# Low parts of the linear-attention input weights: from a VectorE subtract to a negated copy with an adding transfer

## The chip, the cores and the metric

The kernel runs on one core of a Trainium2 chip. The metric is device time in microseconds (us) of one execution; the median of the runs is compared. TensorE (PE) multiplies matrices and PEld is its loading of weights; VectorE (DVE), ScalarE (ACT) and GpSimd (POOL) work elementwise; SyncE (SP) issues most transfers (DMA), ScalarE a few, and GpSimd those that add to what lies at their destination.

## The reference

One inference step of a two-layer decoder with D = 1024, for 512 prompt tokens and 8 decode rows, everything in f32. Layer 0 mixes tokens by windowed attention, layer 1 by gated linear attention (GLA); each is followed by a ConvFFN with 2816 channels and by layer norms. The part that matters here is layer 1's mixer with 4 heads:

```python
def gla_mix(x, s0, w_in, w_a1, w_a2, b_a, norm_g, w_o):
    proj = x @ w_in            # q, k: 128 columns per head; v, g: 256 per head
    ...
    log_a = jax.nn.log_sigmoid(((x @ w_a1) @ w_a2 + b_a).astype(jnp.float32)) / GLA_TAU
    ...
    o, s_new = gla_recurrence(q, k, v, log_a, s0, min(GLA_CHUNK, T))
    o = o * lax.rsqrt(jnp.mean(jnp.square(o), -1, keepdims=True) + NORM_EPS) * norm_g
    o = (o * jax.nn.silu(g)).reshape(B, T, GLA_DV)
    return o @ w_o, s_new
```

## The kernel before

**Products.** Every f32 weight block is split into a high part `wh` (the f32r copy of it) and a low part `wl` (the rest), and so are the activations; a product is high x high, high x low and low x high, three matmuls for each of 8 pieces of the contraction, 24 in all (`product`: lines 231, 233 and 235; line 238 where all low parts stand behind the high parts). The tokens go in two groups, a (256 columns) and b (256 + 8 decode rows).

**Units.** The work is a list of units, each with one weight block of 128 x 1024 values (512 KB). Units 0 to 9 are attention's q, k, v, 10 to 17 its output, 18 to 65 the first ConvFFN (8 single units of gate and value, 18 paired ones, each of which makes one low by transfer in the helper `upper`, and the down-projections), 66 the low-rank decay, **67 to 90 the input weights of the linear attention**, 91 to 98 its output, and from 99 the second ConvFFN. A head of the linear attention has six units: q, k, v0, v1, g0, g1 (67 to 72 are head 0, 73 to 78 head 1, and so on).

**Order.** `order` lets group b follow group a by 4 or 5 units. When b has finished unit u, its slot (6 slots of `wh` and `wl`) is released and `load_next` emits the load of a later unit, `load_unit` (line 175): SP loads the block into one of two raw buffers (184), ScalarE makes the high part (189), and then comes the low part: a VectorE subtract (195), or, for three kinds of units, `low_by_dma` (200, 201), which lets ScalarE write the negated high part and GpSimd issue a transfer that reads the block from DRAM again and adds it. The instructions are not run in the order in which they are emitted: a planner at build time simulates them with its own costs and fixes an order for each engine, so that matmuls of several products can be interleaved. On the chip each engine takes its own list strictly in order.

**Late units.** The first units after a layer norm (here 67 to 71) are marked late; they go through `parts` (line 203), which already uses `low_by_dma` while a norm in certain places is under way (line 211 to 214).

**Around it.** `gla_g` makes the gate: an exponential on ScalarE (1173), plus 1 on GpSimd (`de`, 1174), a reciprocal (1175) and `sg` (1177) on VectorE, which frees the PSUM buffer of the product; later `sg` is scaled by the transposed attention output (1185). `gla_decay` makes the decay (996 to 1014). `gla_sample` advances the states of the decode rows: SP loads values broadcast over the partitions (`vb`, 1155), ScalarE scales the state (1159), VectorE adds the outer product (`sgla`, 1160), SP stores it (1161) and loads the next head's (1019).

Of the kernel before, what the change touches and what calls it, by code (L numbers as in the profile page):

```python
# [99 lines left out]
class Net:  # L100
# [74 lines left out]
    def load_unit(self, u, pieces=1, late=False):  # L175
        src, nt = self.units[u][0], self.units[u][1]
        nc = self.nc
        if nt == 0:
            return self.load_rank(u)
        r = self.raw.tile([P, KD * P], F32, name="raw")  # L180
        h, l = ((self.wx if u == self.extra else self.wts).tile([P, KD * P], F32R, name=name) for name in ("wh", "wl"))
        n = nt * P // pieces
        for c in (slice(i * n, (i + 1) * n) for i in range(pieces)):
            nc.sync.dma_start(out=r[:, c], in_=src[:, c])
            if late:
                self.spawn(self.parts(u, h[:, c], l[:, c], r[:, c], src[:, c]), 1)
                continue
            if u >= HIACT:
                nc.scalar.activation(h[:, c], r[:, c], AF.Copy)  # L189
            else:  # L190
                nc.gpsimd.tensor_scalar(h[:, c], r[:, c], 1.0, 0.0, op0=ALU.mult, op1=ALU.add)
            if self.units[u][2] in (self.ffn_down2, self.ffn_gate, self.ffn_value):
                self.low_by_dma(l[:, c], h[:, c], src[:, c])
            else:
                nc.vector.tensor_tensor(l[:, c], r[:, c], h[:, c].bitcast(F32), op=ALU.subtract)  # L195
        self.w[u] = (h, l)
# [1269 lines left out]
```

## Time and profile before

| | |
|---|---|
| median of 3 runs | 1103.12 us (1101.35 to 1103.88) |
| profiled execution: time / span | 1103.29 us / 1101.5 us |
| mean granted TensorE clock | 0.993 |
| HBM read / written | 153.24 MB / 8.47 MB |

The profile is one execution. The span goes from its first instruction to its last. In rows of instruction groups stand the line, engine, operation, output<-input, shape and count, then busy time and mean (ns), then the idle time of the engine before them and what ended it. In rows of waits: engine, line, what it waited for, us in total, times, longest. In rows of the timeline: start, duration (both us), engine, line, operation, and in brackets the idle time before with its releaser. In rows of windows: the stretch, its length, busy time and instructions of PE, PEld, DVE, ACT and POOL, the granted clock, the share of time in which the 16 transfer engines are busy, and GB/s. Busy time of a matmul is its own duration; matmuls overlap.

### The profile page before, as it was taken

What the parts mean: (1) busy time and instruction counts of PE and PEld (TensorE: products, weight loads), DVE (VectorE), ACT (ScalarE), POOL (GpSimd) and SP (SyncE); (2) the same over time, 40 slices, a digit from 0 to 9 for tenths busy, and PEclk for the clock granted to TensorE, in tenths of its full rate; (3) what the DMA queues carried; (4) which work ended last, traced back from release to release, by engine and by line L of the source; (5) the groups of instructions that cost most, each with busy time, mean ns of one, the idle gap of its engine ahead of it and who ended that gap; (6) DMA issues with size and microseconds to landing.
All of it is one profiled execution on the core that took longest, in us unless ns stands there. A gap on an engine that the chain in (4) does not pass through costs nothing.

```text
span 1101.5 us, 23798 instructions
## 1 busy us (share of the span) xinstructions
PE 1058.3 (96%) x9174; PEld 1030.9 (94%) x9174; DVE 881.2 (80%) x1797; ACT 663.1 (60%) x1308; POOL 308.2 (28%) x512
## 2 busy tenths in 40 slices
PE   8999999899999999999899999999999999999996
PEld 7998899899999999999899899899899999999995
DVE  7897668987778888978667777778987788788975
ACT  5677667866665565647445556467866555655643
POOL 4576562311111110274111100363311111110163
PEclk9999999999999999999999999999999999999998
DMA  7454047687777775438125354558687777774412
GB/s 228 150 171 126 21 135 198 169 193 183 177 181 173 178 166 119 148 106 206 58 74 150 124 177 134 158 172 210 156 192 178 183 174 175 172 190 115 131 50 78
DMA packets 65472, 167.44 MB, mean 152 GB/s; under 512 B 8104, under 2 KB 28624, under 8 KB 65360
## 3 DMA queue, kind: packets, MB, share of 16 engines
q1 hardware_dynamic: 50960, 119.47, 33.7%
q0 software_dynamic: 12240, 44.57, 23.1%
q10 hardware_dynamic: 2160, 1.89, 0.6%
q8 instruction: 72, 1.18, 0.4%
q14 instruction: 40, 0.33, 0.1%
HBM read 153.24 MB, written 8.47 MB: 147 GB/s over the span
## 4 chain that ended last, share of the span: by engine, by line
PE 65%; DVE 13%; DMA 11%; ACT 5%; issue 4%; POOL 1%; SPq 0%; DVEq 0%; ACTq 0%; POOLq 0%
PE widep L303 7%; PE widep L304 7%; PE widep L305 7%; PE accp L231 6%; PE accp L233 6%; PE accp L235 5%; PE widep L898 5%; PE widep L899 5%; PE widep L900 5%; DMA vb<-dv 3%; DMA wl<-in_w_up 3%; DMA raw<-in_w_up 2%; PE accp L917 2%; PE accp L238 1%; PE onep L304 1%
## 5 line engine op out<-in xcount | busy, mean ns | idle before, releaser
L308 ACT ACTIVATE wh<-raw 128x1024 fp32r<-128x1024 f32 x72 | 76.3, 1060 | 103.6 <-PE widep L899 65.8
L189 ACT ACTIVATE wh<-raw 128x1024 fp32r<-128x1024 f32 (+1 forms) x92 | 96.0, 1047 | 59.9 <-PE accp L233 25.9
L303 PE MATMUL widep<-th,wh 128*128 128x264 f32 (+1 forms) x432 | 119.1, 276 | 0.0
L304 PE MATMUL widep<-tl,wh 128*128 128x264 f32 (+1 forms) x432 | 119.1, 276 | 0.0
L305 PE MATMUL widep<-th,wl 128*128 128x264 f32 (+1 forms) x432 | 119.1, 276 | 0.0
L231 PE MATMUL accp<-xh_b,wh 128*128 128x264 f32 x400 | 113.0, 283 | 5.2 <-DVE hprod L801 3.4
L231 PE MATMUL accp<-xs_a,wh 128*128 128x256 f32 x400 | 106.2, 285 | 5.9 <-DVE sg L1177 2.5
L235 PE MATMUL accp<-xh_b,wl 128*128 128x264 f32 x400 | 111.5, 279 | 0.0
L233 PE MATMUL accp<-xl_b,wh 128*128 128x264 f32 x384 | 107.4, 280 | 0.0
L201 POOL DMA_DIRECT2D wl<-in_w_down x28 | 24.3, 868 | 288.3 <-ACT wl L200 276.1
L233 PE MATMUL accp<-xs_a,wh 128*128 128x256 f32 x384 | 103.0, 284 | 0.3
L309 DVE TENSOR_TENSOR wl<-raw,wh 128x1024 fp32r<-128x1024 f32 x72 | 88.2, 1225 | 9.4 <-ACT wh L308 9.3
L195 DVE TENSOR_TENSOR wl<-raw,wh 128x1024 fp32r<-128x1024 f32 (+2 forms) x64 | 79.3, 1247 | 13.4 <-ACT wh L189 12.5
L200 ACT ACTIVATE wl<-wh 128x1024 fp32r<-128x1024 f32 x85 | 89.0, 1050 | 0.9
L827 DVE TENSOR_TENSOR merged<-widep,conv 128x528 f32<-128x528 f32 x72 | 37.4, 562 | 58.3 <-PE widep L305 58.3
L231 PEld LDWEIGHTS accp<-xs_a,wh 128*128 128x128 f32 x400 | 76.7, 195 | 7.7 <-ACT wh L189 3.0
L303 PEld LDWEIGHTS widep<-th,wh 128*128 128x128 f32 x432 | 82.1, 190 | 0.1
L304 PEld LDWEIGHTS widep<-tl,wh 128*128 128x128 f32 x432 | 82.1, 190 | 0.0
L305 PEld LDWEIGHTS widep<-th,wl 128*128 128x128 f32 x432 | 82.1, 190 | 0.0
L231 PEld LDWEIGHTS accp<-xh_b,wh 128*128 128x128 f32 x400 | 75.7, 189 | 6.7 <-DVE hprod L801 4.0
L303 PE MATMUL widep<-xh_b,wh 128*128 128x264 f32 x288 | 79.6, 276 | 0.0
L304 PE MATMUL widep<-xl_b,wh 128*128 128x264 f32 x288 | 79.5, 276 | 0.0
(419 smaller groups left out, 4165.8 us busy)
## 6 DMA issues: line engine op xcount, KB each, us to landing
raw<-in_w_up SPq DMA_DIRECT2D x88, 512.0 KB, 3.9
wl<-in_w_up POOLq DMA_DIRECT2D x52, 512.0 KB, 6.6
raw<-in_w_down SPq DMA_DIRECT2D x44, 512.0 KB, 3.7
wl<-in_w_down POOLq DMA_DIRECT2D x28, 512.0 KB, 6.4
raw<-in_w_gla SPq DMA_DIRECT2D x24, 512.0 KB, 3.5
raw<-in_w_mix_o SPq DMA_DIRECT2D x16, 512.0 KB, 3.9
qs<-hl SPq DMA_DIRECT2D x64, 64.0 KB, 2.1
sgla<-in_state_gla SPq DMA_DIRECT2D x16, 256.0 KB, 3.0
```

Of the source, the lines that this page charges most:

```text
L189: nc.scalar.activation(h[:, c], r[:, c], AF.Copy)
L195: nc.vector.tensor_tensor(l[:, c], r[:, c], h[:, c].bitcast(F32), op=ALU.subtract)
L200: self.nc.scalar.activation(l, h.bitcast(F32), AF.Copy, scale=-1.0)
L231: nc.tensor.matmul(o, h[:, ks], xh, start=k == 0, stop=False)
L233: nc.tensor.matmul(o, h[:, ks], xl, start=False, stop=False)
L235: nc.tensor.matmul(o, l[:, ks], xh, start=False, stop=not tail and k == nt - 1)
L303: self.nc.tensor.matmul(o, h[:, ks], rh, start=k == 0, stop=False)
L304: self.nc.tensor.matmul(o, h[:, ks], rl, start=False, stop=False)
L305: self.final = self.nc.tensor.matmul(o, l[:, ks], rh, start=False, stop=k == KD // 2 - 1).ins
L308: self.nc.scalar.activation(hi, src, AF.Copy)
L309: self.nc.vector.tensor_tensor(lo, src, hi.bitcast(F32), op=ALU.subtract)
L898: nc.tensor.matmul(o, h[:, ks], rh, start=k == 0, stop=False)
```

## The change

The condition on line 192 names the kinds of units whose low part is made by `low_by_dma`. Four kinds are added: the query, key, value and gate units of the linear attention.

```diff
-            if self.units[u][2] in (self.ffn_down2, self.ffn_gate, self.ffn_value):
+            if self.units[u][2] in (self.ffn_down2, self.ffn_gate, self.ffn_value, self.gla_q, self.gla_k, self.gla_v, self.gla_g):
                 self.low_by_dma(l[:, c], h[:, c], src[:, c])
             else:
                 nc.vector.tensor_tensor(l[:, c], r[:, c], h[:, c].bitcast(F32), op=ALU.subtract)
```

The helper that it calls is as before:

```python
def low_by_dma(self, l, h, src):
    self.nc.scalar.activation(l, h.bitcast(F32), AF.Copy, scale=-1.0)
    self.nc.gpsimd.dma_start(out=l, in_=src, accum_op=ALU.add)
```

Units 67 to 71 do not pass line 192. For the others the low part is now made from the high part and DRAM, and the raw buffer is read by the high part's copy alone.

## The prediction

> **What bounds the kernel now.** I read the page's busy shares, then the windows of the stage that the change touches, then what TensorE waits for there.
>
> ```profile
> PE 1058.3 (96%) x9174; PEld 1030.9 (94%) x9174; DVE 881.2 (80%) x1797; ACT 663.1 (60%) x1308; POOL 308.2 (28%) x512
> ```
> ```profile
> core 0: us, PE busy (x) PEld busy (x) DVE busy (x) ACT busy (x) POOL busy (x), PEclk, DMA share, GB/s
> 530.00:690.00 160.00, 154.52 (x1282) 147.40 (x1281) 114.61 (x281) 82.83 (x214) 18.52 (x30) 0.99 0.41 127
> 540.00:550.00 10.00, 7.46 (x44) 6.90 (x43) 7.64 (x17) 5.12 (x15) 4.12 (x9) 0.83 0.24 89
> 586.00:598.00 12.00, 12.00 (x106) 11.90 (x105) 11.32 (x32) 7.93 (x22) 0.87 (x2) 1.00 0.57 173
> 598.00:610.00 12.00, 10.18 (x89) 9.90 (x87) 5.51 (x12) 3.88 (x9) 0.00 (x0) 1.00 0.75 210
> 640.00:650.00 10.00, 8.87 (x79) 8.68 (x79) 5.71 (x16) 4.33 (x10) 0.00 (x0) 1.00 0.73 215
> ```
>
> TensorE (PE) is busy for 96% of the span. In the linear attention (here 530 to 690 us) it is idle for 160 - 154.5 = 5.5 us. Between 540 and 550 us the granted clock is 0.83, worth 10 x 0.17 = 1.7 us. A change to that stage's weights can therefore win about 7 us at most; it can lose more. VectorE (DVE) is at 114.6 of 160 us (72%), ScalarE (ACT) at 52%, and the transfers have 0.41 of their engines. The waits of TensorE between 500 and 690 us, in us, times and longest, are all of these:
>
> ```profile
> PE accp L231 <- DVE sg L1177: 2.5, 1, 2.5
> PE accp L238 <- DMA wl<-in_w_gla: 1.9, 1, 1.9
> PE tp L1065 <- DVE sg L1185: 1.8, 1, 1.8
> PE accp L231 <- ACT wh L189: 1.4, 1, 1.4
> PE tp L1181 <- ACT on L1105: 1.1, 1, 1.1
> ```
>
> Two of the five are for VectorE, and one is already for a low part made by transfer.
>
> **What the change moves.** Each of the 24 units (67 to 90) has one 512 KB weight block. The rows of its low parts and high parts, with count, busy time and mean, and of the transfers that exist already:
>
> ```profile
> L195 DVE TENSOR_TENSOR wl<-raw,wh 128x1024 fp32r<-128x1024 f32 x19 | 23.4, 1229 | 7.2 <-ACT wh L189 6.8 <-PE accp L235 0.3
> ```
> ```profile
> L200 ACT ACTIVATE wl<-wh 128x1024 fp32r<-128x1024 f32 x85 | 89.0, 1050 | 0.9
> ```
> ```profile
> L201 POOL DMA_DIRECT2D wl<-in_w_up x52: 856/865/1028, 154.1 to 1025.4; - x52
> L201 POOL DMA_DIRECT2D wl<-in_w_gla x5: 865/880/881, 501.7 to 515.4; - x5
> ...
> DMA to landing us min/median/max: 5.2/6.6/10.5
> ```
>
> Units 67 to 71 go through another branch, and their five lows are transfers already (x5). The change acts on the other 19. It takes 19 x 1.229 = 23.4 us from VectorE, adds 19 x 1.050 = 20.0 us to ScalarE and 19 x 0.865 = 16.4 us of issuing to GpSimd (POOL), and reads each block a second time. On the transfer engines:
>
> ```profile
> q1 hardware_dynamic: 50960, 119.47, 33.7%
> q0 software_dynamic: 12240, 44.57, 23.1%
> ```
>
> q0 carries the 85 lows: 0.231 x 1101.5 / 85 = 3.0 us of all 16 engines each, so 19 cost 57 us of them. ScalarE rises from 82.8 to about 103 of 160 us, which does not bound it.
>
> *Term 1, VectorE's relief.* The longest wait, 2.5 us before 544.24, ends on a gate (sg) that stands right behind a subtract:
>
> ```profile
> 542.64 1.21 DVE L195 TENSOR_TENSOR wl<-raw,wh 128x1024 fp32r<-128x1024 f32 x1
> 543.77 0.41 DVE L1177 TENSOR_TENSOR sg<-accp,de 128x256 f32<-128x256 f32 x1
> ```
> ```profile
> 544.24 0.53 PE L231 MATMUL accp<-xs_a,wh 128*128 128x256 f32 x1 [2.54 <-DVE sg L1177]
> ```
>
> Without it sg can start 1.2 us earlier. I take 1.2 of the 2.5 us (bounds 0, if the extra ScalarE copy delays the gate's exponential by as much, and 2.5). The clock drop right after this wait, 1.7 us, I take as gone with a wait half as long: -2.9 us in all. The Trainium skill's page "TensorE: Matmul & The Clock Gate", section "HAM oscillation — how this bites in real kernels", says that idle gaps over about 3.4 us bring the slow clock. The trace disagrees: its gap was 2.5 us, and the slow clock followed. By the page's rule the drop would not hang on this gap, the term would be -1.2, and the sum 1.7 us higher.
>
> *Term 2, lows that come late.* A weight slot is freed when group b has done with it; six slots turn round, so unit u waits for b's product of unit u-6, and a's product of u follows soon. For unit 75: the last low matmul of unit 69, the high part, and a's first use of the new low:
>
> ```profile
> 551.46 0.28 PE L235 MATMUL accp<-xh_b,wl 128*128 128x264 f32 x1
> 557.84 0.28 PE L235 MATMUL accp<-xs_a,wl 128*128 128x256 f32 x1
> ```
> ```profile
> 552.06 1.04 ACT L189 ACTIVATE wh<-raw 128x1024 fp32r<-128x1024 f32 x1
> ```
>
> From the slot's release (551.74) to that use is 6.1 us, the shortest of 18 such spans (units 73 to 90; mean 8.3, longest 11.8). The first and the last:
>
> ```profile
> 536.13 0.28 PE L235 MATMUL accp<-xh_b,wl 128*128 128x264 f32 x1
> 544.77 0.42 PE L235 MATMUL accp<-xs_a,wl 128*128 128x256 f32 x1
> ...
> 664.56 0.38 PE L235 MATMUL accp<-xh_b,wl 128*128 128x264 f32 x1
> 672.33 0.28 PE L235 MATMUL accp<-xs_a,wl 128*128 128x256 f32 x1
> ```
>
> The old path needs 0.3 + 1.04 + 1.2 = 2.6 us. The new one needs 0.3 + 1.04 + 1.05 + 0.1 + 6.6 (median landing) = 9.1 us, more than 13 of the 18 spans. In the old order of matmuls TensorE would stand still. But the planner that fixes the order at build time knows that transfers take time, and can run b's product while a's low is missing. It has done so in the first ConvFFN, where b's product (xh_b) runs ahead of a's last low:
>
> ```profile
> 184.34 0.28 PE L235 MATMUL accp<-xh_b,wl 128*128 128x264 f32 x1
> ...
> 188.04 0.38 PE L238 MATMUL accp<-xs_a,wl 128*128 128x256 f32 x2
> ```
>
> What was lost there nevertheless, in the whole run, is the 1.9 us above and
>
> ```profile
> PE accp L238 <- DMA wl<-in_w_up: 2.5, 3, 1.2
> PE accp L235 <- DMA wl<-in_w_up: 0.6, 2, 0.4
> ```
>
> That is 5.0 us over 21 single units whose low is a transfer (52 - 36 of paired units, and 5): 0.24 us each. These are the nearest rows, and 19 x 0.24 = 4.5 us. Bounds: 0 if the planner moves b far enough ahead; if it moves nothing, each stall lengthens the next unit's span by its own length, so about every second unit stalls: 0.4 + 3.0 + 2.1 + 2.9 + 0.1 + 2.1 + 2.4 + 0.2 + 1.6 = 14.8 us. The Trainium skill's page "DMA: Bandwidth & Descriptors", section "Anatomy of one DMA — SWDGE (gpsimd) path", gives 2.0 us plus bytes over 436,000, an estimated 3.2 us for a block; by it the path would be 5.7 us, under every span, and this term 0. The trace disagrees: no landing is under 5.2 us.
>
> *Term 3, the transfers of the decode rows.* VectorE's state updates wait for the broadcast values (vb), and the subtract is not what holds them:
>
> ```profile
> 601.67 0.88 DVE L1160 SCALAR_TENSOR_TENSOR sgla<-vb,kraw,sgla 128x256 f32<-128x256 f32 x2 [3.19 <-DMA vb<-dv]
> 602.47 0.48 DVE L1185 SCALAR_TENSOR_TENSOR sg<-tp,par,sg 128x256 f32<-128x256 f32 x1
> 602.86 1.22 DVE L195 TENSOR_TENSOR wl<-raw,wh 128x1024 fp32r<-128x1024 f32 x1
> ...
> 607.58 0.88 DVE L1160 SCALAR_TENSOR_TENSOR sgla<-vb,kraw,sgla 128x256 f32<-128x256 f32 x2 [3.17 <-DMA vb<-dv]
> 608.38 0.48 DVE L1185 SCALAR_TENSOR_TENSOR sg<-tp,par,sg 128x256 f32<-128x256 f32 x1
> ```
>
> Behind the second wait stands the sg that TensorE waited 1.8 us for. In these 24 us (586 to 610) the transfers are busy for 0.57 x 12 + 0.75 x 12 = 15.8 us; three of the 19 lows fall in them (of units 80 to 82; the last one's subtract is in the fence) and make 15.8 + 9.0 = 24.8 of 24. So vb lands later by part of a low. The same stage of the next head is the 640 to 650 window (0.73), whose 1.1 us wait stands there. The last two heads' stages come when the weights are loaded, or nearly. I take 2.0 us for each of two heads, 4.0 us (bounds 0, if the transfers fit between, and 2 x 3.0 with a clock drop of 1.7 each: 9.4).
>
> *What costs nothing.* GpSimd's issue now waits for the negated copy; behind it in that queue stands de (L1174), the gate's "1 +", for which VectorE's reciprocal waits. POOL is at 12% here and this issue takes 0.9 us, so I give it nothing (1 us per gate if it falls badly, within term 2's bounds). On ScalarE the negated copy pushes what stands behind it by 1.05 us; the two waits of TensorE on ScalarE (1.4, 1.1) could each grow by that, 2.1 us, and I give it nothing because ScalarE has 48% free. SP's load of the next block waited for the subtract to free its raw buffer and now waits for the high part alone, some 1 to 2 us earlier; the load is not the late part, so it wins nothing.
>
> **Sum.** The profiled execution took 1103.29 us (span 1101.5, 1.8 around it), against a median of 1103.12: 1103.3 - 2.9 + 4.5 + 4.0 = 1108.9 us.
>
> **The rivals.**
> *The order stays* (chance 0.18): lows are late in the old order, 14.8 in place of 4.5: 1103.3 - 2.9 + 14.8 + 4.0 = 1119.2. For it: 13 of 18 spans are too short. Against it: the ConvFFN's order above.
> *Faster* (0.24): b's product goes ahead of a's in time. One product is 24 matmuls at 154.52 / 1282 = 0.12 us, 2.9 us, so the mean span grows from 8.3 to 11.2; from 9.1 on no low is late. If vb also finds room, only VectorE's relief counts, now with the whole wait at 544: 1103.3 - 2.5 - 1.7 = 1099.1. Against it: median landing is 6.6 but 10.5 occurs.
> *No change that can be measured* (0.17): what VectorE gains, the two losses eat, at half the size I gave them: 1103.3 - 2.9 + 4.2 = 1104.6.
> *Landings shorter than any row here* (0.02): the path fits all spans, vb is not crowded: 1103.3 - 2.9 = 1100.4. This is what the Trainium skill's formula on "DMA: Bandwidth & Descriptors" would give; no landing bears it out.
>
> **The numbers.** My forecast has the other 0.39. A measurement of this kernel can tell about 0.2%, 2.2 us. Faster: 0.24 + 0.02 = 0.26. Same: 0.17. Slower: 0.39 + 0.18 = 0.57. The range takes in the faster rival's 1099.1 with some tenths below it, 1098.5, and reaches past the stay-in-order case to 1121.0, for one longer landing there. Slower cases alone would be 1105.5 to 1121.
>
> **What would show it.** Term 1: the wait for sg before 544 is shorter, and the slow clock is gone. Term 2: waits "accp <- DMA wl<-in_w_gla" of about 4.5 us, on units above 71; near 15 means the order stayed; none means the faster rival. Term 3: "sgla <- DMA vb" over its present length, DMA share near 1 around 600 us, and the wait behind it on TensorE longer. I am wrong if TensorE's idle time in the stage falls below 5.5 us, or if the lows land in time though the broadcast values do not.

## The result, and the profile after

The change makes the kernel slower: 1116.19 us median (6 runs, 1113.05 to 1122.36) against 1103.18 (6 runs, 1101.05 to 1104.01), a ratio of 1.0128 with a 95% interval of 1.0106 to 1.0150. That is 13.0 us, where 5.6 were forecast. Taken again beside other kernels, as e11 below, it came to 1.0107 (1.0079 to 1.0136). One execution of e1 below (3854.52 us) and two of the kernel before (1359.50 and 1215.35 us) were in a slower state and stand in no ratio. The profiled execution took 1122.36 us (span 1120.6) and was the slowest of its six, 19.1 us over that of before. So the profile shows where the time goes; its microseconds overstate the median's loss.

First the page of the changed kernel: busy time, and the queue that carries the lows.

```profile
PE 1067.1 (95%) x9174; PEld 1036.4 (92%) x9174; DVE 861.2 (77%) x1778; ACT 681.3 (61%) x1327; POOL 316.9 (28%) x531
...
q0 software_dynamic: 14976, 54.53, 27.9%
```

The instruction counts moved as the diff says: 19 fewer on DVE, 19 more on ACT and on POOL. q0 carries 104 lows instead of 85, at 0.279 x 1120.6 / 104 = 3.0 us of all 16 engines each, as before. Now the windows of the stage (the last of these stretches was not shown for the kernel before; its row follows in a fence of its own).

```profile
530.00:690.00 160.00, 145.62 (x1149) 136.10 (x1148) 84.94 (x235) 92.12 (x213) 30.98 (x48) 0.97 0.69 169
540.00:550.00 10.00, 8.57 (x62) 7.43 (x61) 8.11 (x19) 5.81 (x17) 2.69 (x5) 1.00 0.79 156
586.00:598.00 12.00, 10.65 (x88) 10.26 (x87) 11.69 (x33) 9.58 (x23) 3.78 (x7) 1.00 0.72 171
598.00:610.00 12.00, 11.66 (x104) 11.47 (x104) 3.33 (x11) 7.23 (x13) 1.93 (x3) 1.00 0.91 230
...
690.00:750.00 60.00, 56.33 (x466) 52.75 (x465) 42.39 (x89) 28.32 (x69) 18.19 (x24) 0.97 0.48 155
```
```profile
690.00:750.00 60.00, 57.77 (x482) 54.23 (x481) 47.07 (x95) 34.45 (x72) 30.34 (x42) 1.00 0.58 166
```

TensorE's idle time in 530 to 690 us rises from 5.5 to 160 - 145.6 = 14.4 us, and in 690 to 750 from 2.2 to 3.7: 10.3 us more. The transfer engines go from 0.41 to 0.69 busy. The granted clock falls from 0.99 to 0.97 in the first stretch and from 1.00 to 0.97 in the second. The trace of the two stretches holds four windows of 3.413 us at half clock (one from 563.4, two from 662.4, one from 717.0) where before there was one (from 544.3). Three more of them, at 1.7 us each if TensorE has work throughout, are up to 5.1 us. Together up to 15.4 of the 19.1 us. The stage is where the time goes: the last product with the linear attention's input weights ends at 709.0 us instead of 692.5, 16.5 us later, of which 1.5 were lost before unit 67's first low matmul. What lies before the stage and after it is not explained by the change.

The waits of TensorE from 500 to 690 us, as before in us, times and longest:

```profile
PE accp L235 <- DMA wl<-in_w_gla: 8.1, 4, 3.6
PE accp L238 <- DMA wl<-in_w_gla: 2.2, 2, 1.4
PE sc L1045 <- DVE k_a L1037: 2.1, 1, 2.1
PE accp L231 <- ACT wh L189: 1.4, 1, 1.4
...
PE tp L1181 <- ACT on L1105: 0.5, 1, 0.5
```

Waits for low parts are 10.3 us where before they were 1.9, and they sit in six units (71, 72, 75, 79, 85, 87). The two waits for ScalarE that the kernel before has (1.4, 0.5) have not grown. Beyond 690 us there is a new one, 2.0 us before 715.43: it is for a copy of `vk` that stands on ScalarE behind a high part of the output projection, for whose raw block ScalarE had waited 4.0 us. The 2.5 us wait for the gate that was the longest of before is all but gone, and no slow clock stands at 544 us: the gate now runs with no subtract ahead of it.

```profile
543.57 0.41 DVE L1177 TENSOR_TENSOR sg<-accp,de 128x256 f32<-128x256 f32 x1
544.04 0.19 PEld L231 LDWEIGHTS accp<-xs_a,wh 128*128 128x128 f32 x1 [0.45 <-DVE sg L1177]
```

The 2.1 us for `k_a` are new too, and they stand behind a broadcast. The view puts VectorE's wait before the state update down to ScalarE's high part, but the broadcast issued at 606.48 landed 7.6 us later, at 614.04, just before the update:

```profile
614.12 0.88 DVE L1160 SCALAR_TENSOR_TENSOR sgla<-vb,kraw,sgla 128x256 f32<-128x256 f32 x2 [7.12 <-ACT wh L189]
...
615.26 0.42 DVE L1037 TENSOR_TENSOR k_a<-accp,em 128x256 f32<-128x256 f32 x1
```

**One late low, step by step.** The timeline at unit 75, whose span was the shortest before: the last low matmul of unit 69, then high part, negated copy, the issue, b's low matmuls of the next unit, and a's first use.

```profile
551.93 0.28 PE L235 MATMUL accp<-xh_b,wl 128*128 128x264 f32 x1
...
552.13 1.06 ACT L189 ACTIVATE wh<-raw 128x1024 fp32r<-128x1024 f32 x1 [0.93 <-PE accp L233]
...
553.84 1.05 ACT L200 ACTIVATE wl<-wh 128x1024 fp32r<-128x1024 f32 x1
...
555.19 0.89 POOL L201 DMA_DIRECT2D wl<-in_w_gla  x1 [8.28 <-ACT ep L1013]
...
560.00 0.28 PE L235 MATMUL accp<-xh_b,wl 128*128 128x264 f32 x1
...
562.51 0.38 PE L235 MATMUL accp<-xs_a,wl 128*128 128x256 f32 x1 [2.12 <-DMA wl<-in_w_gla]
```

From the slot's release at 552.2 to the use at 562.5 are 10.3 us: 9.1 had been worked out. The landing took 7.3 instead of 6.6, and the copy waited 0.65 us and the issue 0.3 us behind what they need. Before, this span was 6.1. The planner did put b's matmuls in between (up to 560.0), and that was not far enough.

**Where low and broadcast meet.** The end of the third head, 650 to 670 us: the issues of two broadcasts, a state and two lows, then what waits for them.

```profile
650.08 0.69 SPq L1155 DMA_DIRECT2D vb<-dv  x1
...
654.05 0.38 SPq L1019 DMA_DIRECT2D sgla<-in_state_gla  x1
654.11 0.87 POOL L201 DMA_DIRECT2D wl<-in_w_gla  x1 [5.21 <-PE accp L235]
...
656.07 0.87 POOL L201 DMA_DIRECT2D wl<-in_w_gla  x1 [1.09 <-ACT wl L200]
...
656.71 1.13 SPq L1155 DMA_DIRECT2D vb<-dv  x1
...
663.50 0.58 PE L235 MATMUL accp<-xs_a,wl 128*128 128x256 f32 x1 [3.56 <-DMA wl<-in_w_gla]
...
669.53 0.88 DVE L1160 SCALAR_TENSOR_TENSOR sgla<-vb,kraw,sgla 128x256 f32<-128x256 f32 x2 [10.26 <-DMA vb<-dv]
```

The low of unit 87, issued at 654.11, is used at 663.50, 9.4 us later, and TensorE has stood for 3.56 us; VectorE stands 10.26 us for a broadcast. Both wait in the same crowd: the transfer engines are busy for 1.01 to 1.04 of the time in each 5 us from 650 to 665. TensorE then has no wait over 0.25 us until 704 us, so in this execution VectorE's long stand shows in no wait of TensorE; in e11's profile a stand of 10.9 us at the same place shows in one of 2.9 us. Over the stage, VectorE's waits for the broadcasts before and after, and the landings after (minimum, median, maximum in us; before 3.0/4.0/5.8):

```profile
DVE sgla L1160 <- DMA vb<-dv: 14.3, 5, 3.6
```
```profile
DVE sgla L1160 <- DMA vb<-dv: 17.2, 3, 10.3
...
DVE sgla L1160 <- ACT wh L189: 7.1, 1, 7.1
```
```profile
DMA to landing us min/median/max: 3.4/4.7/12.7
```

With the 7.1 us that the view puts down to ScalarE they are 24.3 us, where they were 14.3.

### The profile page after: what moved, and what is told of

The parts are those of the page before. It is cut to its first block, busy times and chain, and to the rows that moved or that the text cites. A ratio compares the mean times of both kernels' runs of the same rounds, so it can differ in the third digit from the quotient of the medians.

```text
span 1120.6 us, 23838 instructions
## 1 busy us (share of the span) xinstructions
PE 1067.1 (95%) x9174; PEld 1036.4 (92%) x9174; DVE 861.2 (77%) x1778; ACT 681.3 (61%) x1327; POOL 316.9 (28%) x531
## 4 chain that ended last, share of the span: by engine, by line
PE 62%; DMA 13%; DVE 11%; ACT 6%; issue 5%; POOL 1%; SPq 0%; DVEq 0%; ACTq 0%; POOLq 0%
PE widep L303 7%; PE widep L305 7%; PE widep L304 7%; PE accp L231 6%; PE accp L233 6%; PE accp L235 5%; PE widep L898 4%; PE widep L900 4%; PE widep L899 4%; DMA wl<-in_w_gla 3%; DMA raw<-in_w_up 2%; DMA wl<-in_w_up 2%; PE accp L917 2%; DMA raw<-in_w_mix_o 1%; PE onep L305 1%
## 5 line engine op out<-in xcount | busy, mean ns | idle before, releaser
L231 PE MATMUL accp<-xs_a,wh 128*128 128x256 f32 x400 | 107.6, 289 | 2.7 <-ACT wh L189 2.7
L200 ACT ACTIVATE wl<-wh 128x1024 fp32r<-128x1024 f32 x104 | 109.2, 1053 | 1.0
L201 POOL DMA_DIRECT2D wl<-in_w_down x28 | 24.3, 866 | 287.9 <-ACT wl L200 287.9
L233 PE MATMUL accp<-xs_a,wh 128*128 128x256 f32 x384 | 104.3, 287 | 0.0
L235 PE MATMUL accp<-xs_a,wl 128*128 128x256 f32 x256 | 74.5, 294 | 9.1 <-DMA wl<-in_w_gla 8.1
```

The lines of the kernel that those rows point to most:

```text
L200: self.nc.scalar.activation(l, h.bitcast(F32), AF.Copy, scale=-1.0)
L231: nc.tensor.matmul(o, h[:, ks], xh, start=k == 0, stop=False)
L233: nc.tensor.matmul(o, h[:, ks], xl, start=False, stop=False)
L235: nc.tensor.matmul(o, l[:, ks], xh, start=False, stop=not tail and k == nt - 1)
```

## The experiments

Two theories were set against each other. **Lateness**: the low's path is longer than the time that the order leaves for it, whatever the transfers do. **Crowding**: the added bytes delay other transfers, the broadcasts `vb` above all, whatever the lows do. Each result is the ratio to the kernel before, timed on the same chip, with its interval. A caution for all of them: each edit also lets the planner choose another order, so two kernels differ in their order as well as in the edit.

**e1, an eighth of the bytes.** In the changed kernel's `low_by_dma`, for the linear attention alone:

```diff
-        self.nc.gpsimd.dma_start(out=l, in_=src, accum_op=ALU.add)
+        self.nc.gpsimd.dma_start(out=l[:, :cols], in_=src[:, :cols], accum_op=ALU.add)
```

(`cols` is 128 for the units 67 to 90 and the whole block for the others.)

> The change, but in the linear attention the transfer adds only the first of the eight pieces of a block (64 KB of 512 KB; the other seven eighths of these low parts lack the weight). ScalarE's negated copy and VectorE's relief stay, the transfer is short and moves an eighth of the bytes. Theory L (the lows come late, and TensorE's slow clock follows the stalls) and theory C (the added bytes crowd the other transfers) both expect the loss to go: 1099 to 1104 us, and none of the waits on wl over 1 us among units 72 to 90. Theory A (ScalarE's 20 us of copies hold up its other work) expects that most of the 13 us stay: over 1110 us.

Measured: 1109.87 (three runs) against 1102.76, 1.0062 (1.0045 to 1.0079). Waits for lows are 1.8 us (10.3 in the change), VectorE's for the broadcasts 20.5. So half of the loss goes with seven eighths of the bytes. That takes away lateness and crowding at once, since a small transfer lands sooner (unit 75's low was used 3.7 us after its issue), and it does not tell them apart. Both theories were wrong about the size: 1099 to 1104 was expected of either, and the time stands at the edge of what theory A named, ScalarE's copies (over 1110). Against A as the main cause stand e12 below, with the same copies and 1105.22, and e15, with all copies and all bytes and less time than its control; that the copies cost some of it is not excluded.

**e2 and e14, bytes without lateness.** The kernel before with its subtract, and for 19 of the 24 units (72 to 90; the late ones do not pass here) a transfer that adds half a block (256 KB) to `scr`, one buffer that nobody reads; e14 is the same with 8 columns (4 KB):

```diff
                 nc.vector.tensor_tensor(l[:, c], r[:, c], h[:, c].bitcast(F32), op=ALU.subtract)
+            if len(self.phases) > 4 and self.phases[3] < u < self.phases[4]:
+                scr = self.scr
+                nc.scalar.activation(scr[:, :8], h[:, :8].bitcast(F32), AF.Copy, scale=-1.0)
+                nc.gpsimd.dma_start(out=scr, in_=src[:, :512], accum_op=ALU.add)
```

> The kernel before, with its VectorE subtract, and beside it, for units 72 to 90, a transfer of half a block (256 KB) that is added into a buffer that nobody reads, behind a tiny ScalarE copy from the high part. No low is late, but half of the added bytes move at the same places. Theory C expects about half of the loss: 1107 to 1111 us, with later vb. Theory L expects less than 3 us: 1102 to 1106 us.

> The half-block run again, but each of the 19 transfers into the unread buffer moves 8 columns (4 KB) in place of 512 (256 KB). If that run's 7 us came from the bytes (theory C), they go: 1101 to 1105 us. If they came from the added instructions and queue places, they stay: 1107 to 1111 us.

Measured: e2 1110.14, 1.0065 (1.0050 to 1.0080); e14 1100.45, 0.9987 (0.9964 to 1.0010). The instructions are the same in both, so the difference, 0.78% or 8.6 us, comes with the bytes. It is not all crowding: the small copy on ScalarE waits until the transfer before it into `scr` has landed, for which ScalarE stands 15.9 us in e2 and 4.1 in e14, with its other work behind it; and the planner's order differs. In e2 TensorE has no wait for a low in its stage. The longest wait in e2 is 2.75 us for a gate that stands on VectorE behind a broadcast (lines are six higher here: 1166 is the update, 1191 the gate); the longest of this kind is 1.0 us in e14 and 1.8 in the kernel before:

```profile
655.59 0.88 DVE L1166 SCALAR_TENSOR_TENSOR sgla<-vb,kraw,sgla 128x256 f32<-128x256 f32 x2 [4.87 <-DMA vb<-dv]
656.39 0.48 DVE L1191 SCALAR_TENSOR_TENSOR sg<-tp,par,sg 128x256 f32<-128x256 f32 x1
...
656.93 0.33 PE L1071 MATMUL tp<-ident,k_b 128*128 128x128 f32 x1 [2.75 <-DVE sg L1191]
```

VectorE's waits for broadcasts are not longer in sum (12.7 us against 15.0 in e14); the longest is (4.9 against 3.1). I read this as crowding that costs time by the one broadcast that comes latest. TensorE's waits for `tp` behind this gate are 3.5 us against 1.7 in e14, a fifth of the 8.6 us; the rest is spread, and how much of it is ScalarE's stand for `scr` was not told apart.

**e3 and e4, b three units behind a instead of four.** In `order`, for the linear attention, in the changed kernel (e3) and the kernel before (e4):

```diff
-                lead = max(LAG, min(top, p0 + 2 * top - u))
+                lead = max(3 if p0 == self.phases[3] else LAG, min(top, p0 + 2 * top - u))
```

> The change, and in the linear attention group b follows group a by 3 units in place of 4, so that a weight slot is freed one unit earlier and a low has about 8 us more to land. Theory L expects most of the loss to go: 1100 to 1107 us, waits on wl of the units above 71 under 3 us in all. Theory C expects no help: over 1112 us.

> The kernel before with the same smaller lag, as the control of the run beside it. Both theories expect 1101 to 1107 us: the old low path needs 2.6 us and was not late; a shorter lag can cost where b's work waits for a's.

Measured: e3 1116.56, 1.0127 (1.0106 to 1.0148); e4 1110.73, 1.0074 (1.0057 to 1.0091). The slot comes free a unit earlier and the waits for lows fall to 1.5 us, but the time does not. The order by itself costs 0.74%, and against that control the change still loses half a per cent (5.8 us, where it lost 13.0 and, taken again, 10.7). So the lag did take away about half of the loss, and cost as much itself. What TensorE waits for in e3:

```profile
PE tp L1065 <- DVE sg L1185: 6.0, 2, 3.6
...
PE accp L235 <- DMA wl<-in_w_gla: 1.2, 1, 1.2
```

The gate stands where lows were waited for, by the same chain as in e2: VectorE stands 7.13 us for a broadcast until 652.47, and TensorE 3.58 us, until 654.87, for the gate behind it. Of e4's loss, most stands near the output projection (690 to 750 us), where TensorE waits 4.1 us for a split of the gated output and the clock is at 0.94.

**e5 and e6, a second broadcast buffer.** In the changed kernel (e5) and the kernel before (e6):

```diff
-            vb = self.gp.tile([P, 2, 256], F32, name="vb")
+            vb = self.gp.tile([P, 2, 256], F32, name="vb", bufs=2)
```

> The change, with two buffers in place of one for the broadcast values vb of the decode rows, so that the next load need not wait until VectorE has used the one before. Theory C (the added transfers make vb later, VectorE's list stands still behind it and TensorE with it) expects most of the loss to go: 1103 to 1110 us, VectorE's waits for vb under 8 us. Theory L (TensorE waits for the lows themselves, and its clock drops) expects no more than 3 us: 1112 to 1117 us.

> The kernel before with the same two buffers, the control of the run beside it. VectorE's waits for vb should fall from 17 us to under 8; of TensorE's waits at most the 1.8 and 1.1 us can go: 1099 to 1104 us.

Measured: e5 1114.25, 1.0109 (1.0087 to 1.0131); e6 1104.01, 1.0012 (0.9997 to 1.0028). The broadcast can now be issued a use ahead, and VectorE's wait is gone; the lows' is not:

```profile
PE accp L235 <- DMA wl<-in_w_gla: 7.6, 5, 2.0
PE accp L238 <- DMA wl<-in_w_gla: 2.3, 3, 1.1
```
```profile
DVE sgla L1160 <- DMA vb<-dv: 2.0, 2, 1.1
```

The time lies within both intervals of the change itself. So the wait for the broadcasts, removed alone, is worth nothing that can be measured; against its control, e6, the change still loses 10.2 us.

**e7 and e8, low matmuls behind the high ones.** Group a's product takes its low parts after all high parts (line 238) in the whole stage, which puts the first use of a low about 1.8 us later within its product:

```diff
-        behind = self.units[u][2] == self.ffn_down and g.i == 0 or g.i == 0 and nt == KD and not tail and any(e < u < e + LOWS for e in (*self.phases[2:4], *self.phases[5:6]))
+        behind = self.units[u][2] == self.ffn_down and g.i == 0 or g.i == 0 and nt == KD and not tail and (self.phases[3] < u < self.phases[4] or any(e < u < e + LOWS for e in (*self.phases[2:4], *self.phases[5:6])))
```

> The change, with the eight low matmuls of group a's products behind the sixteen high ones for all units 67 to 90 (so far for 67 to 72 alone). A low then has 16 x 0.11 = 1.8 us more to land, and nothing else of the work changes. Theory L expects waits on wl to fall from 10.3 us to under 4, and 1107 to 1112 us. Theory C expects no change: over 1113 us.

> The kernel before with the same order within group a's products, the control of the run beside it. The old lows were not late, so both theories expect no change over 3 us: 1100 to 1106 us.

Measured: e7 1118.32, 1.0155 (1.0122 to 1.0188); e8 1101.11, 0.9990 (0.9977 to 1.0003). The changed kernel waits 10.2 us for lows, 8 times, as much as without the edit. The slack was not there on the chip, so the time, which lies where the crowding theory had it, does not speak against lateness. I read this as the planner having used it up in a new order; that was not tested by itself.

**e9 and e10, six units by transfer.** The kernel before with the transfer for six units alone: those with long spans (e9) or short ones (e10).

```diff
-            if self.units[u][2] in (self.ffn_down2, self.ffn_gate, self.ffn_value):
+            if self.units[u][2] in (self.ffn_down2, self.ffn_gate, self.ffn_value) or u in (74, 77, 82, 83, 88, 89):
```

For e10 the units are 75, 80, 81, 84, 85 and 86.

> The kernel before, with six more lows made by transfer: units 74, 77, 82, 83, 88 and 89, whose spans from the slot's release to group a's first use of the low were the longest (8.9 to 11.8 us). Theory L: the new path of 9.1 to 9.5 us nearly fits, so 1101 to 1105 us and waits on wl of units above 71 under 1.5 us. Theory C: the same bytes as in the run beside it, so the same time as there.

> The same with six units whose spans were the shortest but one (75, 80, 81, 84, 85, 86: 6.1 to 7.0 us). Theory L: each is 2.5 to 3.4 us too short, so 1105 to 1111 us and waits on wl of units above 71 of 3 us or more. Theory C: the same time as the run beside it, within 2 us.

Measured: e9 1109.05, 1.0057 (1.0037 to 1.0078); e10 1117.47, 1.0147 (1.0129 to 1.0166). Neither came out as the lateness theory had it: e9 was to be 1101 to 1105 with waits for lows under 1.5 us and has 4.5, e10 is slower than 1111. The same bytes cost 8.4 us more where the spans are short, but that is not lateness alone, for e10's waits for lows are 3.2 us, fewer than e9's. The short units also stand where the broadcasts are loaded: three of those near 600 and 650 us take 5.3 to 6.3 us to land in e10 and at most 4.2 in e9, and VectorE waits 22.1 us for broadcasts in e10, 13.4 in e9. So the two runs differ in crowding too. The loss of e10 stands in part in gates (of L1177's 3.2 us, 2.5 are the wait that the kernel before has too), and in four windows of slow clock in its stage (one in e9):

```profile
PE accp L231 <- DVE sg L1177: 3.2, 2, 2.5
PE tp L1065 <- DVE sg L1185: 2.8, 1, 2.8
PE accp L235 <- DMA wl<-in_w_gla: 2.7, 3, 1.4
PE tp L1181 <- DVE sg L1185: 2.1, 1, 2.1
```

The gate of 2.8 us stands behind a wait of VectorE of 5.1 us for one of these broadcasts. A second reading, that a low which the planner expects late is paid in the order that makes room for it, is argued and not shown.

**e13, lateness without bytes.** The kernel before, its subtract kept, but for the six short units GpSimd multiplies the raw block by 1 three times ahead of it (3 x 1.09 us, and what these wait for):

```diff
+                for _ in range(3 if u in (75, 80, 81, 84, 85, 86) else 0):
+                    nc.gpsimd.tensor_scalar(r[:, c], r[:, c], 1.0, 0.0, op0=ALU.mult, op1=ALU.add)
                 nc.vector.tensor_tensor(l[:, c], r[:, c], h[:, c].bitcast(F32), op=ALU.subtract)
```

> The kernel before, with its VectorE subtract; for units 75, 80, 81, 84, 85 and 86 GpSimd, which is idle, first multiplies the raw block by 1 three times (about 2.1 us each, after the high part is made), so that the low comes about 6 us later, with no transfer and no ScalarE copy added. Theory L: about the loss of e10_short6, 1109 to 1117 us. Theory C: no loss over 3 us, 1101 to 1106 us.

Measured: 1109.48 against 1101.65, 1.0063 (1.0044 to 1.0082). With no byte added the loss is some 7 us, and only 1.3 us of it is a wait for a low. The waits for gates are no longer in sum than in the kernel before (2.5 us for `tp` in both, lines are two higher), they stand in another place:

```profile
PE tp L1067 <- DVE sg L1187: 2.5, 1, 2.5
...
PE accp L237 <- DVE wl L197: 1.3, 1, 1.3
```

But most of the loss does not show where the lows are late. In the profile (6.9 us over that of before in span) the last product with the linear attention's input weights ends 1.9 us later than before (694.4 against 692.5), and 5.2 us are lost between there and the first product of a paired unit in the second ConvFFN (804.9 against 797.8). In the change itself 16.5 us are lost by that end and 0.9 between the two. So e13 shows that the kernel with later lows is slower, but not that the lateness is what costs it: the order that the planner chose behind them (which may also have put work behind that end) is a rival that was not told apart, and so is GpSimd's load, as it also makes the gates' 1 + exp.

**e11, the change again.**

> The change as it is, for a second profile: its first profiled execution was the slowest of six. 1113 to 1119 us; waits on wl of 6 to 10 us, in the same places, since the order of the matmuls is fixed.

Measured: 1111.69 (1110.43 to 1119.13), 1.0107 (1.0079 to 1.0136). This is a little under the range expected; in the waits the picture is the same: for lows 8.1 us, for broadcasts 20.1, the longest landing of one 13.3. The profiled execution was again the slowest, 1119.13.

**e12, an eighth of the bytes and two broadcast buffers.**

> The transfer of one eighth of each block (the other seven eighths of the linear attention's lows lack the weight) with two vb buffers. If the 7 us that the eighth alone cost come from VectorE's waits for vb, they go: 1101 to 1105 us. If they come from ScalarE's copies and the planner's order, they stay: 1108 to 1112 us.

Measured: 1105.22 against 1100.99, 1.0038 (1.0023 to 1.0052). That is just over the range for the first case. With an eighth of the bytes and two buffers 0.38% remain, where the change has 1.28 and 1.07; but e1 and e12 differ by less than their intervals allow to tell, so that VectorE's waits for `vb` were e1's loss is not shown.

**e15 and e16, both waits taken away.** The edits of e3 and e5 together, in the changed kernel (e15) and the kernel before (e16).

> The change with lag 3 and two vb buffers: no low is late, and VectorE does not stand behind vb. If lateness and vb are the whole loss, the same time as the control beside it within 3 us. If bytes crowd something else too, 4 us or more over it.

> The control of the run beside it: the kernel before with lag 3 and two vb buffers. 1106 to 1113 us, as lag 3 alone cost 8 us, and two vb buffers changed little.

Measured: e15 1105.84, 1.0029 (1.0012 to 1.0047); e16 1109.20, 1.0066 (1.0044 to 1.0088). What is left in e15 of TensorE's longest waits, and its stage:

```profile
PE accp L238 <- DMA wl<-in_w_gla: 1.5, 2, 1.0
PE accp L231 <- ACT wh L189: 1.4, 1, 1.4
```
```profile
530.00:690.00 160.00, 156.66 (x1304) 148.84 (x1305) 102.04 (x261) 103.66 (x235) 31.47 (x50) 1.00 0.76 196
```

With all bytes of the change (DMA share 0.76, more than in the change itself) TensorE is idle for 3.3 us in the stage and the clock is full. In the time of the changed kernel each edit alone gained nothing that can be measured; together they bring it from 1.0128 and 1.0107 to 1.0029, 8 to 11 us. In this order the change is 3.4 us faster than its control.

**e17 and e18, the lag of 3 in the middle alone.** As e15 and e16, but with the lag of 3 for the first 19 units, since e4 lost its time near the output projection:

```diff
-                lead = max(3 if p0 == self.phases[3] else LAG, min(top, p0 + 2 * top - u))
+                lead = max(3 if p0 == self.phases[3] and u < p0 + 20 else LAG, min(top, p0 + 2 * top - u))
```

> The change with two vb buffers, and b's products three units behind a's in the first 19 units of the linear attention alone; in its last units they are four behind again, as in the change. Two causes (the lows' lateness and the crowded vb), with VectorE's relief left once both are gone: the lag of 3 throughout cost the kernel before about 10 us near the out projection, so that here the change should come below its own 1105.84 with lag 3 throughout and below its control with the same order: 1098 to 1102, and faster than its control by 0.2 to 0.5%. If the gain of the lag came from the order near the end instead, this run stays at 1106 or above; if the last units' lows (87 among them) carry the lateness, waits on wl come back there, 3 us or more, and it stands at 1104 to 1108.

> The kernel before with the same order and two vb buffers, the control. VectorE's subtracts stay. If the out projection's loss was the price of the lag of 3 there, this comes to 1101 to 1105 (the kernel before with two vb buffers was 1104.01, with lag 3 as well 1109.20). If the order after the middle makes no difference, it is again at 1108 to 1110.

Measured: e17 1111.06 against 1101.02, 1.0085 (1.0063 to 1.0106); e18 1103.69, 1.0021 (1.0006 to 1.0037). The control came out as expected, the change did not: it was to be the fastest of all, and it stands 7.4 us over its control. The lows of the last units were another case named (1104 to 1108 us), and it is one of them, 87 again:

```profile
648.71 0.38 PE L235 MATMUL accp<-xs_a,wl 128*128 128x256 f32 x1 [3.72 <-DMA wl<-in_w_gla]
```

It was issued at 639.5 and used 9.2 us later; the transfers are busy for 0.91 of the time from 640 to 645 us and for 1.07 from 645 to 650. TensorE's waits for lows are 4.8 us in e17 and 0.2 in e18, and e17 has one more window of slow clock in the stage. But e18 has waits of its own that e17 lacks (5.2 us for gates, 3.3 for `vk`), so this does not account for the 7.4 us, and they stay open. No version that has the change was faster than the kernel before.

## Why the prediction was right in direction and wrong in size

**The path and its spans: right.** 9.1 us were worked out; units 75, 79 and 85, which TensorE waited for, took 10.3, 9.3 and 9.5, unit 87 in the crowd 13.3; the landings are 6.7 us in the median (6.6).

**Term 2, the late lows: the step that failed.** It priced a late low at 0.24 us, the mean over 21 units of other stages, and came to 4.5 us. Measured were 10.3 - 1.9 = 8.4 us more of waits for lows in the profile (6.2 in e11's), in six units, of which one alone has 3.6 and another 2.1. The mean was taken over units that mostly had slack, while here 13 of 18 spans were too short by the prediction's own count; its upper bound, 14.8, was worked from these spans and was the better row to go by. And the term counted only waits that name a low; whether lateness is paid in the new order as well, as e10 and e13 may suggest, is not shown.

**The clock: wrong sign.** Term 1 took 1.7 us as gained because the wait at 544 us would go. It went, with its slow window. But new ones came behind other waits (three follow the waits for the lows of units 75 and 87, one the wait for `vk` at 715 us): four windows instead of one in the profile, up to 5.1 us more, in e11 two. The prediction added the clock to the wait that it removed and not to those that it added, except at a bound.

**Term 1, VectorE's relief: right as far as it can be seen.** The wait for the gate at 544 us is 0.45 us of the weight load, where a matmul stood for 2.5. What it is worth with both losses gone, e15 against e16 puts at 3.4 us, near the 2.9 forecast. Since the planner's orders differ (e16 waits 3.8 us near 700 us for something that e15 does not wait for), and e17 against e18 shows no gain, this is a sign and not a measurement of the term.

**Term 3, the broadcasts: the mechanism right, its size not settled.** Foreseen: broadcasts later by part of a low, a transfer share near 1 around 600 us, and 4.0 us. The share there is 0.91, the broadcast that landed at 614.04 took 7.6 us where the median before was 4.0, and VectorE's waits grew by 10 us; the worst place for VectorE was 650 to 670 us, behind the second of the two that were named. TensorE's waits in the stage behind a broadcast grew by less: 1.8 us before (a gate), 2.1 in the change (`k_a`), 4.3 in e11. Bytes without late lows, e2 against e14, cost 8.6 us with half a block each, but part of that may be ScalarE's stand for `scr`.

**The sum.** Terms 2 and 3 were added as if independent. In the time of the changed kernel, taking away either alone gives nothing (e3 1.0127 and e5 1.0109 against 1.0128 and 1.0107), taking away both gives 8 to 11 us (e15). But the edits change the kernel before as well; lag 3 costs it 0.74%. Against the kernel before with the same edit, the loss goes with the waits that are left (waits from 500 to 710 us as the views name them, loss from the medians, all in us; in the first row 7.1 and 6.4 us more of waits for broadcasts are put down to ScalarE):

| the change | TensorE's waits for lows | VectorE's waits for broadcasts | loss against the same edit |
|---|---|---|---|
| as it is; again (e11) | 10.3; 8.1 | 19.5; 20.1 | 13.0; 10.7 |
| low matmuls behind (e7, e8) | 10.2 | 22.4 | 17.2 |
| two buffers (e5, e6) | 9.9 | 2.0 | 10.2 |
| lag 3 (e3, e4) | 1.5 | 14.8 | 5.8 |
| lag 3 in the middle, two buffers (e17, e18) | 4.8 | 1.0 | 7.4 |
| lag 3, two buffers (e15, e16) | 1.5 | 1.5 | -3.4 |

So lateness alone taken away halves the loss, the broadcasts alone leave most of it, and both together take all of it in one order (e15); in another (e17), with 4.8 us of waits for lows left, 7.4 us remain. And the low of unit 87 lands late in the crowd, so that the two causes are partly one. That the two together make the loss is what these runs speak for; what each contributes is not shown, since every row has an order of its own.

**The rivals.** "The order stays" gave 1119.2, nearer in size, by a mechanism that did not happen: at unit 75 b's matmuls were moved ahead. "Faster" and "no change" need lows in time and room for the broadcasts; the profile has neither. The planner did lengthen the 18 spans, from a mean of 8.3 to 12.0 us, more than the 11.2 that "faster" reckoned with, but not where it was needed: units 83, 88 and 89 got 17 to 22 us, units 75, 79 and 85 only 9.3 to 10.3. What was given nothing (ScalarE, GpSimd, SP) shows in no longer wait of TensorE for ScalarE up to 690 us, and the one of 2.0 us for `vk` beyond it stands behind a late raw block; on the low's path of unit 75, copy and issue came 0.65 and 0.3 us later than with no queue ahead of them.

**Open.** Why six short units alone (e10) cost as much as all 19; how much of e13's loss is GpSimd, how much the order behind the lows; how the 13 us divide between the causes; what the planner's order makes of each edit, which no run holds fixed; and why both profiled executions of the change are 6 to 7 us above its median.

## What to carry to other kernels

To replace an engine's work by a transfer, compare the new path with the span of each single place, and price the places whose span is too short from those spans, not by a mean over others that had slack. When a change makes one thing late and crowds another, remove each alone and then both, and set each run beside a control with the same edit: an edit that takes a loss away and costs as much itself looks like a loss that was free. And count the clock with every wait that a change may add, as much as with the one that it takes away.

## What the runs showed of the hardware

**The slow clock goes by windows of a fixed grid, and half-empty ones are enough.** In the changed kernel's profile the slow stretches begin at 563.4, 662.4 and 717.0 us: 99.0 and 54.6 us apart, 29 and 16 times 3.413. Each pair below is a grid window and the one after it (second column: length; third: TensorE's busy time; then, behind POOL, the granted clock):

```profile
560.00:563.40 3.40, 1.28 (x12) 1.08 (x11) 0.19 (x1) 0.00 (x0) 2.77 (x5) 1.00 0.91 225
563.40:566.80 3.40, 3.40 (x18) 3.40 (x17) 0.00 (x0) 0.00 (x0) 0.00 (x0) 0.50 0.46 90
...
703.30:706.70 3.40, 1.77 (x17) 1.57 (x16) 1.60 (x4) 0.52 (x1) 0.00 (x0) 1.00 0.96 357
706.70:710.10 3.40, 3.40 (x30) 3.28 (x29) 2.37 (x3) 2.59 (x5) 0.47 (x1) 1.00 0.56 171
713.60:717.00 3.40, 1.57 (x12) 1.27 (x13) 1.93 (x4) 1.78 (x3) 0.00 (x0) 1.00 0.41 152
717.00:720.40 3.40, 3.40 (x15) 1.85 (x13) 3.10 (x6) 0.03 (x1) 0.48 (x1) 0.50 0.50 164
```

A window that was 0.38 or 0.46 busy is followed by half clock, one that was 0.52 busy is not. Laid over all 20 profiles of this case, every full-clock window under 0.43 (54 of them) was followed by a slow one and, of those over 0.58, none, but for one place near 135 us (0.78 to 0.84, in 11 profiles), which stays open; between 0.43 and 0.58 both occur. By this, the same short wait costs up to 1.7 us more or nothing, as it falls on the grid. The Trainium skill's page "TensorE: Matmul & The Clock Gate", section "What's actually happening", has a free-running window of 3413 ns; the trace agrees with that. It asks for an idle window, and its section "HAM oscillation — how this bites in real kernels" for gaps over about 3.4 us; here a gap of 2.1 us (before 562.51, in the first window above) was enough.

**An adding transfer lands late in a crowd.** The low of unit 87 landed 9.4 us after its issue in the change and 9.2 in e17, with the transfer engines busy for 1.01 to 1.04 of the time from 650 to 665 us and for 0.91 and 1.07 in the two stretches of e17, against 6.6 to 7.3 us from issue to use for units 75, 79 and 85, which were waited for as well.
